# A batched matmul (A times B transposed) on one core: the last 256 KB of output stored in three transfers of unequal spread instead of inside one

## The chip, the cores and the metric

The kernel runs on one core of a Trainium2 chip. The metric is the device time of one execution in microseconds (us); lower is better. Before the change the median of 15 runs is 125.15 us (124.88 to 125.45).

## What is computed

Sixteen independent products of float32 matrices, each 512 by 512:

```python
batch, m, k, n = 16, 512, 512, 512
np.matmul(a, b.transpose(0, 2, 1)).astype(np.float32)
```

The inputs are 33.55 MB, the output is 16.78 MB.

## The kernel before

**Tiling and stages.** The batches are worked in eight pairs (`pairs`), and `J = 4` output rows of a batch belong to each of the 128 partitions: row `p * 4 + j` of a batch lies in partition `p`, place `j`. A load (L87) brings both batches of a pair of `a` or of `b`, 2 MB, into one of seven slots of `ld`; even numbers are `a`, odd ones `b`. DVE casts to bf16 (`ha`, `wa`, `hb`, `wb`), PE transposes against an identity into `tp` (L199), ACT and DVE bring the transposes to `ta` (L157) and `tb` (L144), PE multiplies into `ps` (L218), and ACT copies the product to `ob` (L177), one of seven slots of 128 partitions by 4 rows by 512 float32. So a partition's share of a batch is four rows of 2 KB, 8 KB that lie side by side in `ob` and in the output.

**Queues.** ACT issues all loads but number 1, which SP issues; after that SP issues the stores, one per batch, 1 MB each. ACT's loads and SP's stores are two queues over the same 16 DMA engines. SP waits for `s_out` ahead of each store; ACT raises it on the second batch of a pair, after its first and after its last copy, so that store `2u` may go when the first copy of batch `2u + 1` is done, and store `2u + 1` when its last is.

**The end of the program**, which the change touches. `store(n)` (L92 to L96) waits and issues one transfer of a whole batch, whose semaphore `s_st[n % 7]` rises by 16 when all of it has landed. The loop at L107 issues stores 0 to 14, inside a hand-ordered block that closes with a barrier of all engines (L40). A second block (L232 to L234) then makes ACT wait for the landings of stores 9 to 14, one `wait_ge` for each. The last store, of batch 15, is issued by SP outside the block (L236); it is tied to the block only in the order of issue, so SP issues it while ACT waits. Its landing is waited for by SP itself, in the program's closing section (L270). That closing wait of SP asks for two things: the landing of the last store, and a semaphore of ACT that ACT raises after its walk through its own waits and a drain (L232). After it come drains and two barriers of all engines.

Of the kernel before, what the change touches and what calls it, by code (L numbers as in the profile page):

```python
# [10 lines left out]
def kernel(  # L11
# [6 lines left out]
    nc = tc.nc  # L18
    P = 128
    batch, M, K = a.shape  # L20
    _, N, _ = b.shape
    J = M // P
# [7 lines left out]
    NO = 7  # L30
# [3 lines left out]
    def sbuf(name, shape, dtype):  # L34
        return ctx.enter_context(nc.sbuf_tensor(name, shape, dtype))

    def sem(name):
        return tc.alloc_semaphore(name)

    with tc.tile_critical(no_gpsimd_drain=True):  # L40
# [8 lines left out]
        ob = sbuf("ob", [P, NO, J, N], f32)  # L49
# [4 lines left out]
        s_ld = [sem(f"s_ld{i}") for i in range(NL)]  # L54
        s_st = [sem(f"s_st{i}") for i in range(NO)]

        s_go = sem("s_go")
        s_wa = sem("s_wa")
        s_wb = sem("s_wb")
# [9 lines left out]
        s_out = sem("s_out")  # L69
# [5 lines left out]
            out=ident[:], in_=ident[:], compare_op=mybir.AluOpType.not_equal, fill=1.0,  # L75
# [13 lines left out]
        def landed(n):  # L89
            return s_st[n % NO], 16 * (n // NO + 1)  # L90

        def store(n):  # L92
            nc.sync.wait_ge(s_out, n + 1)
            nc.sync.dma_start(
                out[n].rearrange("(p j) n -> p j n", j=J), ob[:, n % NO]
            ).then_inc(landed(n)[0], 16)  # L96

        load(0, nc.scalar)
        load(1, nc.sync)
# [4 lines left out]
            nc.gpsimd.wait_ge(s_ld[n % NL], 16 * (n // NL + 1)).then_inc(s_go, 1)  # L104

        nc.sync.wait_ge(s_ld[0], 32)
        for n in range(batch - 1):  # L107
            store(n)

        def taker(engine):  # L110
            return lambda s, n: engine.wait_ge(s, n).then_inc(s, -n)  # L111
# [9 lines left out]
        with nc.Fori(0, pairs, engines=[dve]) as u:  # L121
            for x, (h, w, s_c, s_w) in enumerate(
# [4 lines left out]
                if x == 0:  # L127
# [4 lines left out]
                    out=h[:, J:, :], in_=src[:, J:, :HK]  # L132
                ).then_inc(s_c, 1)
                nc.vector.tensor_copy(out=w[:], in_=src[:, :, HK:]).then_inc(s_w, 1)  # L134
            for ko in range(KO):
# [5 lines left out]
                if ko == 1:  # L141
# [3 lines left out]
                    out=tb[:, ko, :],  # L145
# [7 lines left out]
        for u in range(pairs):  # L153
            for ko in range(KO):
                nc.scalar.wait_ge(s_ta, KO * u + ko + 1)
                for e in range(2):
                    c = nc.scalar.copy(  # L157
                        out=ta[:, ko, e * J * P:(e + 1) * J * P].rearrange(
                            "k (j p h) -> k j p h", j=J, h=2
                        ),  # L160
# [10 lines left out]
            for e in range(2):  # L171
                n = 2 * u + e
                if n >= NO:
                    nc.scalar.wait_ge(*landed(n - NO))
                for j in range(J):
                    nc.scalar.wait_ge(s_mm, J * n + j + 1)
                    c = nc.scalar.copy(  # L177
                        out=ob[:, n % NO, j, :].rearrange("m (p j) -> m p j", j=2 * J),
# [51 lines left out]


    with tc.tile_critical(sync_engine=act, no_gpsimd_drain=True):  # L232
        for n in range(batch - NO, batch - 1):
            nc.scalar.wait_ge(*landed(n))  # L234
    waits = nc.cur_bb.bb.instructions[-1]
    last = nc.sync.dma_start(  # L236
        out[batch - 1].rearrange("(p j) n -> p j n", j=J), ob[:, (batch - 1) % NO]
    )
    tc.add_manual_dep(
        last.ins,  # L240
        waits.name,
# [33 lines left out]
```

## Time and profile before

| what | value |
|---|---|
| median of 15 runs | 125.15 us |
| the profiled execution, its own time | 125.18 us |
| its span, first to last instruction | 123.4 us (1.78 us of its time lie around it) |
| PE, PEld, DVE, ACT busy | 92.3, 57.4, 68.0, 68.0 us |
| moved by DMA | 50.34 MB, 408 GB/s over the span |
| share of 16 DMA engines' span, load queue and store queue | 60.5% and 36.3% |
| last copy to `ob` (L177) starts, lasts | 114.49 us, 0.59 us |
| store 14 and the last store issued by SP | 112.95 and 115.26 us |

PE is the TensorE matmul, DVE VectorE, ACT ScalarE, SP SyncE; a "q" behind an engine's name is its instruction sequencer, which waits and issues. The profile shows busy shares in 40 slices, the chain of work that ended last, groups of instructions by line, waits by who waited for whom, and the DMA share and rate in any stretch. The trace also holds every DMA packet with its start, length and size, though not the number of the engine that moved it, and the moment of every count of a store's semaphore.

### The profile page before, as it was taken

Reading aid. Unit: us, or ns where it says so; the run is one execution under the profiler, and the core shown is the slowest. Engines: PE = TensorE matmul, PEld = TensorE weight load, DVE = VectorE, ACT = ScalarE, POOL = GpSimd, SP = SyncE. Lnnn points to the kernel's source line nnn. Section 1 sums busy time; section 2 is a strip of 40 time slices with the busy share of each in tenths; the row PEclk is TensorE's granted clock in tenths of the full one; section 3 lists DMA queues with packets and bytes.
Section 4 is the critical chain, followed back from the end, with each engine's and each line's share of the span. In section 5 each row is a group of like instructions: output and inputs, shape, how many; then the busy total and the mean of one; then the engine's idle time right before and its main releaser. Section 6 shows DMA issues by size and latency. Waiting matters only on the chain. (4 is left out here: it accounts for less than half of the span.)

```text
span 123.4 us, 2235 instructions
## 1 busy us (share of the span) xinstructions
PE 92.3 (75%) x768; PEld 57.4 (47%) x768; DVE 68.0 (55%) x96; ACT 68.0 (55%) x130; POOL 0.7 (1%) x6
## 2 busy tenths in 40 slices
PE   0000089999899999989998999899899926999000
PEld 0000079546734774476467447634764515844000
DVE  0000598891898389568928991891977039510000
ACT  0400063557956885596679658946976093655300
POOL 2000000000000000000000000000000000000000
PEclk9999999999999999999999999999999998699955
DMA  4999999999999999999999999999999999999990
GB/s 122 398 430 441 430 425 425 441 425 436 425 425 425 425 398 388 446 422 436 420 428 446 409 422 452 406 452 430 414 446 420 414 422 428 428 425 422 433 422 19
DMA packets 4609, 50.34 MB, mean 408 GB/s; under 512 B 512, under 2 KB 512, under 8 KB 512
## 3 DMA queue, kind: packets, MB, share of 16 engines
q10 hardware_dynamic: 2160, 31.46, 60.5%
q1 hardware_dynamic: 2448, 18.88, 36.3%
q14 instruction: 1, 0.01, 0.0%
HBM read 33.55 MB, written 16.78 MB: 408 GB/s over the span
## 5 line engine op out<-in xcount | busy, mean ns | idle before, releaser
L218 PE MATMUL ps<-tb,ta 128*128 128x512 bf16 x256 | 57.7, 379 | 0.4
L177 ACT COPY ob<-ps 128x512 f32<-128x512 f32 x64 | 34.3, 591 | 27.3 <-PE ps L218 24.3
L157 ACT COPY ta<-tp 128x512 bf16<-128x512 bf16 x64 | 33.0, 613 | 15.8 <-PE tp L199 15.2
L218 PEld LDWEIGHTS ps<-tb,ta 128*128 128x128 bf16 x256 | 24.1, 98 | 30.5 <-issue 3.9
L199 PE MATMUL tp<-ident,ha 128*128 128x128 bf16 x256 | 20.3, 236 | 18.4 <-PEq L111 17.9
L199 PEld LDWEIGHTS tp<-ident,ha 128*128 128x128 bf16 x256 | 17.3, 106 | 22.0 <-issue 20.2
L144 DVE COPY tb<-tp 128x1024 bf16<-128x1024 bf16 x32 | 21.3, 685 | 5.2 <-DVEq L111 5.2
L199 PE MATMUL tp<-ident,hb 128*128 128x128 bf16 x256 | 18.8, 232 | 3.3 <-PEq L111 3.3
L199 PEld LDWEIGHTS tp<-ident,hb 128*128 128x128 bf16 x256 | 16.7, 105 | 4.0 <-issue 3.7
L130 DVE CAST ha<-ld 128x1024 bf16 x8 | 5.5, 690 | 14.7 <-POOLq L104 13.7
L139 DVE COPY ha<-wa 128x2048 bf16<-128x2048 bf16 x8 | 5.5, 691 | 12.7 <-DVEq L111 12.7
L134 DVE CAST wa<-ld 128x2048 bf16 x8 | 9.8, 1220 | 0.0
L134 DVE CAST wb<-ld 128x2048 bf16 x8 | 9.8, 1220 | 0.0
L130 DVE CAST hb<-ld 128x1024 bf16 x8 | 5.5, 688 | 7.5 <-DVEq L111 7.5
L143 DVE COPY hb<-wb 128x2048 bf16<-128x2048 bf16 x8 | 5.5, 685 | 0.1
L131 DVE CAST ha<-ld 128x1024 bf16 x8 | 5.5, 686 | 0.0
L131 DVE CAST hb<-ld 128x1024 bf16 x8 | 5.5, 686 | 0.0
L152 ACT ACT_TABLE_LOAD x1 | 1.3, 1283 | 4.0 <-issue 4.0
L74 POOL TENSOR_SCALAR_AFFINE_SELECT ident<-ident 128x128 bf16<-128x128 bf16 x1 | 0.3, 292 | 0.2 <-POOL ident L72 0.2
L72 POOL MEMSET ident<- 128x128 bf16 x1 | 0.2, 204 | 0.5 <-SPq L40 0.5
L152 ACT COPY one<-const-float32-1.0 128x1 f32<-128x1 f32 x1 | 0.2, 192 | 0.0
L259 POOL MEMSET const-bfloat16-1.0<- 128x1 bf16 x1 | 0.1, 101 | 0.0
(3 smaller groups left out, 0.3 us busy)
## 6 DMA issues: line engine op xcount, KB each, us to landing
ld<-in_a_dram ACTq DMA_DIRECT2D x8, 2048.0 KB, 28.3
out_dram<-ob SPq DMA_DIRECT2D x16, 1024.0 KB, 25.4
ld<-in_b_dram ACTq DMA_DIRECT2D x7, 2048.0 KB, 26.0
ld<-in_b_dram SPq DMA_DIRECT2D x1, 2048.0 KB, 12.5
```

The costliest lines, as they stand in the source:

```text
L74: nc.gpsimd.affine_select(out=ident[:], in_=ident[:], compare_op=mybir.AluOpType.not_equal, fill=1.0, base=0, pattern=[[-1, P]], channel_m ...
L130: nc.vector.tensor_copy(out=h[:, :J, :], in_=src[:, :J, :HK])
L131: nc.vector.tensor_copy(out=h[:, J:, :], in_=src[:, J:, :HK]).then_inc(s_c, 1)
L134: nc.vector.tensor_copy(out=w[:], in_=src[:, :, HK:]).then_inc(s_w, 1)
L139: nc.vector.tensor_copy(out=ha[:], in_=wa[:]).then_inc(s_ca, 1)
L143: nc.vector.tensor_copy(out=hb[:], in_=wb[:]).then_inc(s_cb, 1)
L144: nc.vector.tensor_copy(out=tb[:, ko, :], in_=tp[:, 2 + ko % 2].rearrange("k j p -> k (j p)"),).then_inc(s_eb, 1)
L152: nc.scalar.copy(out=one[:], in_=nc.const_aps.tensor(1.0, (P, 1), f32))
L157: c = nc.scalar.copy(out=ta[:, ko, e * J * P:(e + 1) * J * P].rearrange("k (j p h) -> k j p h", j=J, h=2), in_=tp[:, ko % 2, :, e * HP:(e ...
L177: c = nc.scalar.copy(out=ob[:, n % NO, j, :].rearrange("m (p j) -> m p j", j=2 * J), in_=ps[:, j, :].rearrange("m (j p) -> m p j", j=2 * J),)
L199: t = nc.tensor.transpose(tp[:, 2 * x + g, j, :], h[:, j, g * P:(g + 1) * P], ident[:])
L218: t = nc.tensor.matmul(ps[:, j, :], ta[:, ko, (e * J + j) * P:(e * J + j + 1) * P], tb[:, ko, :].rearrange("k (j p) -> k j p", j=2 * J)[:, ...
```

## The change

The first three rows of each partition of batch 15 now go as a transfer like the others, with the semaphore of their slot, at the end of the loop. The fourth row of each partition, 2 KB in each of 128 partitions, goes in three transfers by groups of partitions: 92 to 127 (36 partitions, over twelve DMA engines), 0 to 31 (32, over sixteen), both issued by SP at once behind the loop, each with a semaphore of its own, and 32 to 91 (60, over fifteen) as the last store, where the whole batch's stood. ACT's block of waits has three more: the landing of batch 15's first three rows, and of the two new transfers.

```diff
+        s_part = [sem(f"s_part{i}") for i in range(2)]
...
-        def store(n):
-            nc.sync.wait_ge(s_out, n + 1)
-            nc.sync.dma_start(
-                out[n].rearrange("(p j) n -> p j n", j=J), ob[:, n % NO]
-            ).then_inc(landed(n)[0], 16)
+        def store(n, lo=0, hi=J, part=slice(0, P)):
+            return nc.sync.dma_start(
+                out[n].rearrange("(p j) n -> p j n", j=J)[part, lo:hi], ob[part, n % NO, lo:hi]
+            )
...
-        for n in range(batch - 1):
-            store(n)
+        for n in range(batch):
+            nc.sync.wait_ge(s_out, n + 1)
+            store(n, hi=J if n < batch - 1 else J - 1).then_inc(landed(n)[0], 16)
+
+        for s, part in zip(s_part, (slice(92, P), slice(0, 32))):
+            store(batch - 1, lo=J - 1, part=part).then_inc(s, 16)
...
-        for n in range(batch - NO, batch - 1):
+        for n in range(batch - NO, batch):
             nc.scalar.wait_ge(*landed(n))
+        for s in s_part:
+            nc.scalar.wait_ge(s, 16)
     waits = nc.cur_bb.bb.instructions[-1]
-    last = nc.sync.dma_start(
-        out[batch - 1].rearrange("(p j) n -> p j n", j=J), ob[:, (batch - 1) % NO]
-    )
+    last = store(batch - 1, lo=J - 1, part=slice(32, 92))
```

## The prediction

> **What bounds the kernel now.** I read the page's slices first, then the end in fine windows, then who waits there. The slices:
>
> ```profile
> PE   0000089999899999989998999899899926999000
> ...
> DMA  4999999999999999999999999999999999999990
> GB/s 122 398 430 441 430 425 425 441 425 436 425 425 425 425 398 388 446 422 436 420 428 446 409 422 452 406 452 430 414 446 420 414 422 428 428 425 422 433 422 19
> ```
>
> The DMA engines are full from the second slice to the last but one at 390 to 450 GB/s, while PE has gaps at both ends. So the kernel is bound by its 50.34 MB, and a compute engine matters only if it starves the queues. At the end it can't: the last copy to `ob` ends at 115.08 us, the last store is issued at 115.26, and its first packets start at about 117.9, behind the stores before it. What is left is how the engines finish. Windows of the end (the columns after the clock, which is 0.50, are the DMA share and GB/s):
>
> ```profile
> 119.00:120.00 1.00, 0.00 (x0) 0.00 (x0) 0.00 (x0) 0.00 (x0) 0.00 (x0) 0.50 1.04 442
> ...
> 120.25:120.50 0.25, 0.00 (x0) 0.00 (x0) 0.00 (x0) 0.00 (x0) 0.00 (x0) 0.50 0.26 98
> ...
> 120.75:121.00 0.25, 0.00 (x0) 0.00 (x0) 0.00 (x0) 0.00 (x0) 0.00 (x0) 0.50 0.08 33
> ...
> 121.25:121.50 0.25, 0.00 (x0) 0.00 (x0) 0.00 (x0) 0.00 (x0) 0.00 (x0) 0.50 0.08 33
> 121.50:121.75 0.25, 0.00 (x0) 0.00 (x0) 0.00 (x0) 0.00 (x0) 0.00 (x0) 0.50 0.08 33
> ```
>
> 33 GB/s is one 8 KB packet in a quarter of a microsecond: from 120.75 on a single engine works. The trace's packets say the same. Fifteen engines end their data between 120.26 and 120.86; one **trailing engine** starts its last packet at 121.60 and ends it at 121.91, so it is 1.05 us behind the next. The counts of the last store follow: fifteen from 120.62 to 121.22, the sixteenth at 122.38. Store 14 has the same spread, 118.17 to 119.91. The end is then this:
>
> ```profile
> SPq L270 <- DMA out_dram<-ob: 6.7, 1, 6.7
> ...
> L270 SPq EVENT_SEMAPHORE  x1: 28/28/28, 122.4 to 122.4; - x1
> ```
>
> SP's closing wait lasts 6.7 us, ends at 122.40 with the trailing engine's count, and the drains and barriers behind it take 1.0 us to 123.4. The other condition of that wait, ACT's semaphore, was met long before. ACT's end (L234, then the lines of L270 and L232 on ACT's sequencer; count, length in ns, first and last start):
>
> ```profile
> L234 ACTq EVENT_SEMAPHORE  x1: 17/17/17, 119.9 to 119.9; - x1
> ...
> L270 ACTq EVENT_SEMAPHORE  x5: 38/38/38, 120.0 to 120.3; - x5
> L270 ACTq COMPARE_BRANCH  x1: 33/33/33, 120.4 to 120.4; - x1
> ...
> L232 ACTq DRAIN  x1: 14/14/14, 120.6 to 120.6; - x1
> ```
>
> This is the row that decides my forecast. L234 ends at 119.93, when store 14 lands (119.91). By its semaphore that is the wait for store 14, the one written **last** in the loop; the waits for stores 13, 12, 11, 10 and 9 come after it, in that reversed order, one to each of the five instructions of L270, which start 0.077 us apart, each together with a wait of the program's own. Then come the branch, an event at L232 and the drain that raises ACT's semaphore at 120.62. From the landing to there is 0.71 us. Before the change this walk is free: it ends 1.76 us ahead of the last store's landing.
>
> **The change part by part.**
>
> *Issues on SP.* One transfer becomes four: 3 more issues at 0.333 us (the row of L94 and L236) and some 0.05 between them. The first three rows go when the last copy is done, at about 115.1, the two parts at 115.5 and 115.9. Then SP arrives at the barrier of L40, at about 116.25 where it came at 113.32; DVE, PE, POOL and ACT wait there but have no work left. The last part goes at about 116.7. The engines need the parts only after the first three rows, from 119.6 on, and the part that is issued last not before 120.0. The cover is 3 us; the first load's packets came 1.04 us after its issue. Cost: nothing, and without the cover 1.2 us at most.
>
> *The packets.* A 16 KB packet takes 0.611 us and an 8 KB packet 0.309, so 8 KB cost 0.302 and a packet 0.007; it starts 0.003 before its predecessor ends. A 6 KB row group is then 0.231 and a 2 KB row 0.080 (an estimate; the trace has nothing between 4 B at 0.009 and 8 KB at 0.309, and these are its bounds). Before, the trailing engine has 8 packets of 8 KB in the last store, 8 x 0.306 = 2.45 us. After, it has 8 of 6 KB, 1.85, and its rows of the three parts: 36 / 12 = 3 rows if it is among the twelve, 2 of the sixteen for certain, 60 / 15 = 4 if it is among the fifteen. The trace doesn't number engines, so all combinations are open. What counts is the part over all sixteen (`s_part[1]`), which no engine escapes: without the twelve's rows ahead of it, it ends 1.85 + 0.16 = 2.01 us after the trailing engine starts batch 15, **0.44 earlier** than before, landing at 121.94; with them 0.24 later, at 122.19. The fifteen's rows stand behind it and end at 122.05 + 0.47 (from last packet to count, as before) = 122.5 at worst, and only SP waits for them.
>
> [...]
>
> *The other fifteen engines.* At most 9 rows in place of 8 quarter shares: 0.08 us, and two more count packets of 0.009. That brings the latest of them from 120.86 to about 120.96; the cover is the trailing engine's lag of 1.05 us. Reading 36 or 32 partitions at once instead of 128 may slow them: between nothing and, if two engines share what one had, a doubling of the nine rows, 0.72 us, to 121.68. I take nothing, as no row shows a slowing; even the doubling stays within the lag, so the sum doesn't change.
>
> [...]
>
> *ACT's waits.* Three more: batch 15's first rows, `s_part[0]`, `s_part[1]`. If the order is reversed as it is now, ACT stands at `s_part[1]`, whose last count is the trailing engine's, and everything else comes after it, satisfied but not free: the 0.71 of before, and three waits more, two to an instruction of 0.077: 0.08 to 0.15, I take 0.12. Together **0.83 us, now on the path**, since SP's closing wait asks for ACT's semaphore. Bounds of the walk: 0.33 if the new wait stands last (0.71 less five steps of 0.077), 0.94 if each new wait takes an instruction. I take 0.83 because the row shows the reversed order.
>
> *Sum.* 121.94 + 0.83 = 122.77, and 0.02 for SP to see it: 122.79 in place of 122.40, so +0.39 us. The span becomes 123.8 and the execution 125.18 + 0.39 = 125.57; the profiled execution is 0.03 over the median, so I forecast 125.55.
>
> **The rivals.**
>
> 1. *The trailing engine is one of the twelve.* For it: they are twelve of sixteen. Against it: nothing in this trace. `s_part[1]` lands at 122.19, the walk ends at 123.02, SP at 123.04: +0.64, 125.8.
> 2. *The waits are walked in the written order*, `s_part[1]` last, and all others are done by then. For it: the program is written so. Against it: L234, which shows store 14's wait first. Then 121.94 + 0.33 + 0.02 = 122.29, -0.11: 125.05, not slower. The point from which it decides is a walk of 0.44 us behind the landing, the gain of the packets: shorter is a gain, longer a loss.
> 3. *Faster.* As 2, and the trailing engine's count comes 0.36 us after its last packet, as the other engines' counts do, in place of 0.47, or its small rows cost less than I take: -0.22 to -0.35, 124.8 to 124.95. Against it: it needs both. With the reversed order it would need a landing 1.1 us earlier, and only 0.44 us of work is taken from the trailing engine.
> 4. *The change doesn't do what it says*: the parts spread otherwise, so that the trailing engine keeps 8 or 9 rows. That gives the price of 1.
>
> **How the numbers follow.** Forecast (the trailing engine outside the twelve, reversed walk) 0.58; rival 1 with 4 0.17; rival 2 0.15; rival 3 0.10. About 0.2%, 0.25 us, is what a measurement of this kernel can tell from no change; the forecast is 0.15 us beyond it, and with the walk's bounds and the rows' price I give it 0.85 of being slower by more. So slower 0.58 x 0.85 + 0.17 = 0.66, same 0.09 + 0.15 = 0.24, faster 0.10. The forecast's own range is 125.35 to 125.7 (walk 0.71 to 0.94, landing 121.9 to 122.0). The range for 8 in 10 leaves out rival 3 and the upper part of rival 1: 124.95 to 125.9.
>
> **What would show it.** In the profile after: SP's closing event (L270) at about 122.8, and before it on ACT one single wait that ends at 121.9 to 122.0, then six or seven events 0.077 apart; SP's wait ended by ACT and no longer by the DMA. The windows from 120.75 on should show smaller packets and the single engine done by about 121.5. Rival 1 shows that engine at work until 121.7 or later; rival 2 shows ACT's last event, not its first, ending with the landing. I am wrong if ACT's semaphore is raised within 0.4 us of the last landing, or if the trailing engine lands more than 0.8 us earlier.

## The result

The changed kernel takes 125.80 us (median of 9 runs, 125.68 to 126.13) against 125.16 before (47 runs, 124.86 to 125.67): ratio 1.0053, 95% interval 1.0042 to 1.0063, so 0.66 us longer, 0.53 to 0.79. A second set beside other kernels gave 1.0047 (1.0034 to 1.0061). The direction, and ACT's walk as the cause of it, were as forecast; the relief of the trailing engine was not there, and the size was that of the first rival (125.8) and not that of the forecast (125.55).

### The profile page after: what moved, and what is told of

Its sections match the earlier page's. It is cut to its first block, busy times and chain, and to the rows that moved or that the text cites. A ratio compares the mean times of both kernels' runs of the same rounds, so it can differ in the third digit from the quotient of the medians.

```text
span 123.8 us, 2239 instructions
## 1 busy us (share of the span) xinstructions
PE 91.0 (74%) x768; PEld 55.9 (45%) x768; DVE 67.9 (55%) x96; ACT 68.0 (55%) x130; POOL 0.7 (1%) x6
## 5 line engine op out<-in xcount | busy, mean ns | idle before, releaser
L203 PE MATMUL tp<-ident,ha 128*128 128x128 bf16 x256 | 19.0, 228 | 18.0 <-PEq L115 17.6
L203 PEld LDWEIGHTS tp<-ident,ha 128*128 128x128 bf16 x256 | 16.3, 102 | 21.5 <-issue 19.7
L203 PE MATMUL tp<-ident,hb 128*128 128x128 bf16 x256 | 18.3, 229 | 3.5 <-PEq L115 3.3
L203 PEld LDWEIGHTS tp<-ident,hb 128*128 128x128 bf16 x256 | 16.1, 103 | 4.4 <-issue 4.1
```

Of the source, the lines that this page charges most:

```text
L203: t = nc.tensor.transpose(tp[:, 2 * x + g, j, :], h[:, j, g * P:(g + 1) * P], ident[:])
```

## The profile after

The profiled execution took 125.59 us, span 123.8, so 0.41 over the profiled execution of before and 0.21 under the median of its own kernel. In the changed kernel L274 is the program's closing section (L270 before), L238 ACT's written waits (L234) and L236 the block around them (L232).

The DMA rows of the page, after (DMA busy tenths and GB/s in 40 slices):

```profile
DMA  4999999999999999999999999999999999999990
GB/s 106 397 439 429 429 429 434 445 429 434 424 429 424 424 392 408 432 413 455 408 424 455 410 439 432 410 445 424 434 429 421 426 429 424 426 421 426 432 375 9
```

Nothing changed up to the last two slices: the four issues on SP left no gap in the DMA engines. The end in windows, after:

```profile
119.00:120.00 1.00, 0.00 (x0) 0.00 (x0) 0.00 (x0) 0.00 (x0) 0.00 (x0) 0.50 0.98 399
120.25:120.50 0.25, 0.00 (x0) 0.00 (x0) 0.00 (x0) 0.00 (x0) 0.00 (x0) 0.50 0.74 279
120.75:121.00 0.25, 0.00 (x0) 0.00 (x0) 0.00 (x0) 0.00 (x0) 0.00 (x0) 0.50 0.06 25
121.25:121.50 0.25, 0.00 (x0) 0.00 (x0) 0.00 (x0) 0.00 (x0) 0.00 (x0) 0.50 0.07 25
121.50:121.75 0.25, 0.00 (x0) 0.00 (x0) 0.00 (x0) 0.00 (x0) 0.00 (x0) 0.50 0.07 25
121.75:122.00 0.25, 0.00 (x0) 0.00 (x0) 0.00 (x0) 0.00 (x0) 0.00 (x0) 0.50 0.02 8
```

Most of the other engines end a little later (279 GB/s from 120.25 on, where it was 98; the last of them ends at 120.82, at 120.86 before), and from about 120.8 one engine is alone, as before. 25 GB/s is three packets of 2 KB in a quarter of a microsecond: the trailing engine works on the fourth row until 121.84, where it was done at 121.91 before. The trace's packets give its share: after its last 6 KB packet (end 121.10) come 3 rows, a count, 2 rows, a count, 4 rows, a count. **It has all three parts**, nine rows of 2 KB in place of eight quarters. The counts land at 121.84 (`s_part[0]`), 122.05 (`s_part[1]`) and 122.30 (the last store). It is the rows that show the share, not the moment: in changed_again's trace below the engine has the same 3, 2 and 4 rows, but is less behind there (store 14 lands at 119.46, 119.71 here), and `s_part[1]` lands at 121.81.

Who waits, after: first a line of the waits of SP, then ACT's end and SP's closing events (count, lengths in ns, first and last start):

```profile
SPq L274 <- ACTq L236: 5.7, 1, 5.7
```

```profile
L238 ACTq EVENT_SEMAPHORE  x2: 38/38/38, 121.9 to 122.1; - x2
...
L274 ACTq EVENT_SEMAPHORE  x5: 38/38/38, 122.1 to 122.5; - x5
L274 ACTq COMPARE_BRANCH  x1: 32/32/32, 122.5 to 122.5; - x1
...
L236 ACTq DRAIN  x1: 8/8/8, 122.8 to 122.8; - x1
...
L274 SPq EVENT_SEMAPHORE  x1: 480/480/480, 122.3 to 122.3; - x1
```

The releaser of SP's closing wait was the last store and is now ACT. SP stands 0.48 us in that wait after its own transfer has landed (122.30), from 122.32 to 122.80. In that time ACT walks: its second written wait, `s_part[1]`, ends at 122.07; then follow the five events, the branch, an event and the drain, 0.72 us from the landing to ACT's semaphore at 122.77.

## The experiments

Theory A: the loss is ACT's walk, which now begins when the last part lands, and the trailing engine isn't relieved. Theory B: the loss is in the transfers, by small packets, few partitions at once or more issues. Ratios are to the kernel before, run beside on the same chip.

**walk_alone**: the walk without the parts. All stores are whole and in the loop, there is no last store outside it.

```diff
-        for n in range(batch - 1):
+        for n in range(batch):
             store(n)
...
-        for n in range(batch - NO, batch - 1):
+        for n in range(batch - NO, batch):
             nc.scalar.wait_ge(*landed(n))
```

> All sixteen stores are issued whole in the loop and ACT's block waits for all seven last landings; no transfer is split, and SP has no last store of its own to wait for. Theory A (the loss is ACT's walk through its waits, which now begins only when the last transfer lands): the landing stays where it was before, at 122.4 us of the span, and the walk of 0.72 us, as it stood behind the landing of s_part[1] in the changed kernel (122.05 to 122.77), follows it: 0.7 over before, about 125.85. Theory B (the loss is in the transfers: small packets, fewer partitions at once, four issues): nothing is split, so 125.15 to 125.25.

Measured: 1.0058 (1.0042 to 1.0075), 0.73 us over. Its SP waits, and the end of ACT:

```profile
SPq L260 <- ACTq L232: 8.4, 1, 8.4
```

```profile
L234 ACTq EVENT_SEMAPHORE  x1: 38/38/38, 122.3 to 122.3; - x1
...
L232 ACTq DRAIN  x1: 8/8/8, 123.0 to 123.0; - x1
```

The whole store lands at 122.32, as before within 0.06; ACT's semaphore comes at 123.04, 0.72 later. No transfer is split and the loss is there: theory B is out as the main cause.

**parts_alone**: the parts without the walk. The kernel before, with its last store replaced by the changed kernel's four transfers, all outside ACT's block:

```diff
-    last = nc.sync.dma_start(
-        out[batch - 1].rearrange("(p j) n -> p j n", j=J), ob[:, (batch - 1) % NO]
-    )
+    for lo, hi, p0, p1 in ((0, 3, 0, 128), (3, 4, 92, 128), (3, 4, 0, 32), (3, 4, 32, 92)):
+        last = nc.sync.dma_start(
+            out[batch - 1].rearrange("(p j) n -> p j n", j=J)[p0:p1, lo:hi],
+            ob[p0:p1, (batch - 1) % NO, lo:hi],
+        )
```

> The same four transfers as in the changed kernel, but all issued behind ACT's block, where the last store stood, so that SP waits for their landings and ACT waits for stores 9 to 14 only, as before. Theory A: the walk is off the path again; the trailing engine moves the same bytes in more packets (nine rows of 0.080 us for eight quarters of 0.305, and three more counts, +0.13 us), and SP's closing wait is one or two events of 0.07 longer: 0.1 to 0.25 over before, about 125.3. Theory B: as slow as the changed kernel, about 125.8.

Measured: 1.0017 (1.0005 to 1.0028), 0.21 us over. SP's waits and events at the end:

```profile
SPq L272 <- DMA out_dram<-ob: 4.8, 3, 4.4
```

```profile
L272 SPq EVENT_SEMAPHORE  x3: 28/28/28, 122.0 to 122.4; - x3
```

SP waits for the DMA again, and its last event comes at 122.44, 0.02 after the last landing (122.43). The trailing engine has 3, 2 and 4 rows here too. So the split costs a little and gains nothing: its relief isn't there.

**waits_turned**: the changed kernel with ACT's waits written the other way round.

```diff
-        for n in range(batch - NO, batch):
-            nc.scalar.wait_ge(*landed(n))
-        for s in s_part:
-            nc.scalar.wait_ge(s, 16)
+        for s in reversed(s_part):
+            nc.scalar.wait_ge(s, 16)
+        for n in reversed(range(batch - NO, batch)):
+            nc.scalar.wait_ge(*landed(n))
```

> The changed kernel with ACT's nine waits written in the opposite order, so that s_part[1] is the last to be walked. Theory A: 0.33 us stand behind the landing of s_part[1] in place of 0.72, which is only 0.07 later than SP sees the landing of the last transfer (0.26 behind s_part[1]): about 0.4 under the changed kernel, 125.4. Theory B: the order of waits is nothing, 125.8 as changed.

Measured: 1.0031 (1.0017 to 1.0045), 0.39 us over before. Its five last waits on ACT, and the drain that raises ACT's semaphore:

```profile
L274 ACTq EVENT_SEMAPHORE  x5: 173/610/2417, 116.5 to 121.8; - x5
...
L236 ACTq DRAIN  x1: 8/8/8, 122.2 to 122.2; - x1
```

The waits are now spread over the last transfers (up to 2.4 us in one of them, waiting for a landing) and not strung behind them. `s_part[1]` lands at 121.94 and ACT's semaphore comes at 122.24, 0.31 later; the last store lands at 122.19, so SP would have stood there almost as long anyway. The point estimate is 0.27 us under the changed kernel's, for a new order of nine lines; the two intervals meet at 1.0042 to 1.0045, and the two were not run side by side.

**which_engine**: which engine trails? Changed kernel, parts of other sizes (with a third semaphore in `s_part`):

```diff
-        for s, part in zip(s_part, (slice(92, P), slice(0, 32))):
+        for s, part in zip(s_part, (slice(0, 7), slice(7, 15), slice(15, 80))):
...
-    last = store(batch - 1, lo=J - 1, part=slice(32, 92))
+    last = store(batch - 1, lo=J - 1, part=slice(80, P))
```

> The fourth row of each partition goes in parts of 7, 8, 65 and 48 partitions, whose largest divisors up to sixteen are 7, 8, 13 and 16. If a part runs on that many engines from the lowest-numbered on, the trailing engine's 2 KB packets tell its place: 1, 1, 5, 3 rows if it is among the first seven, 0, 1, 5, 3 if it is the eighth, 0, 0, 5, 3 if it is the ninth to thirteenth, 0, 0, 0, 3 if it is one of the last three. The changed kernel's trace shows 3, 2 and 4 rows on it, so it is not one of the last four, by this rule. One look; the time is not the question.

Measured (a single execution, 125.54): the trailing engine's packets are 8 of 6 KB, then 1, 1, 5 and 3 rows. It is one of the seven engines of the smallest part.

**which_engine_2**: as parts_alone, with other parts:

```diff
+    for lo, hi, p0, p1 in ((0, 3, 0, 128), (3, 4, 0, 1), (3, 4, 1, 3), (3, 4, 3, 7), (3, 4, 7, 128)):
```

> As which_engine, with parts of 1, 2, 4 and 121 partitions (over 1, 2, 4 and 11 engines by their divisors), issued behind ACT's block so that the walk is off the path. The rows on the trailing engine, which is among the lowest seven, tell more: 1, 1, 1, 11 if it is the first, 0, 1, 1, 11 the second, 0, 0, 1, 11 the third or fourth, 0, 0, 0, 11 the fifth to seventh. Eleven rows in place of eight make it 0.24 to 0.5 later than before. One look.

Measured (a single execution, 125.49, on another chip): its rows are 0, 0, 0 and 11, and its trace has 530 count packets, 18 more than that of the kernel before, as many as 1, 2, 4 and 11 engines make. The trailing engine is not one of the four, and it is one of the eleven. If it is the same engine in both runs and the parts nest, it is the fifth, sixth or seventh in the order in which they take engines in. In the changed kernel's trace they nest: its packets after the 6 KB ones, linked where one begins 2 to 6 ns before another ends, make sixteen engines, of which twelve have 3, 2 and 4 rows, three 2 and 4, and one 2. That the smaller parts here do so too was not shown. A number is a place in that order: no trace gives an engine's own.

**even_parts** and, beside the changed kernel, **even_parts_again**: all three parts over sixteen engines.

```diff
-        for s, part in zip(s_part, (slice(92, P), slice(0, 32))):
+        for s, part in zip(s_part, (slice(80, P), slice(0, 48))):
...
-    last = store(batch - 1, lo=J - 1, part=slice(32, 92))
+    last = store(batch - 1, lo=J - 1, part=slice(48, 80))
```

> The changed kernel with its three parts over all sixteen engines each: partitions 80 to 127 (48), 0 to 47 (48) and 48 to 79 (32, the last store), so that every engine has 3, 3 and 2 rows, the eight quarters it had before. Theory A (the trailing engine has all three parts, and ACT's walk stands behind s_part[1]): s_part[1] comes after 6 rows and not 5, so 0.08 later, and the rest is as changed: 125.75 to 125.9. Rival C (the unequal spread relieves the trailing engine, and the loss would be greater without it, by the six rows of 0.08): 126.2. Rival D (fewer partitions or fewer engines at once cost time): under the changed kernel by 0.2 or more, 125.5.

> The changed kernel as it is, beside the next run on one chip: 0.5% over before, as it was.

> even_parts once more, beside the changed kernel. Theory A: 0.0 to 0.1 us over the changed kernel. Rival D (fewer engines or partitions at once cost time): 0.2 or more under it.

Measured: even_parts 1.0043 (1.0018 to 1.0068); even_parts_again 1.0046 (1.0032 to 1.0060) beside 1.0047 (1.0034 to 1.0061) for the changed kernel. The spread over twelve, sixteen and fifteen engines makes no difference that these runs can tell: it doesn't relieve the trailing engine (rival C asked for about 1.008), and no cost of it is seen (rival D asked for 1.0031 or less, just under the second interval but inside the first, so a small cost is not excluded).

**pool_share**: a try to relieve it. Behind ACT's block, rows 0 and 1 in one transfer, rows 2 and 3 in parts, two of them issued by POOL:

```diff
+    for engine, lo, hi, p0, p1 in (
+        (nc.gpsimd, 2, 4, 0, 7), (nc.gpsimd, 2, 4, 7, 70), (nc.sync, 0, 2, 0, 128),
+        (nc.sync, 2, 4, 70, 80), (nc.sync, 2, 4, 80, 128),
+    ):
```

> A try to relieve the trailing engine in earnest. Rows 2 and 3 of the last batch (4 KB pieces of 0.155 us) go in parts: 7 and then 63 partitions issued by POOL, 10 and 48 by SP; rows 0 and 1 of all partitions by SP; all behind ACT's block, so that SP waits for the landings. If POOL's transfers take their engines in turn from where the last one stopped (7 engines, then the nine others), the first seven engines have 1 + 3 + 1 = 5 pieces and the nine others 10 or 11, in place of 8: the trailing engine ends 3 x 0.155 = 0.46 earlier, less 0.1 for counts and closing events, 124.8 against 125.15 before. If POOL's parts lie otherwise, or POOL's way of issuing costs something at the end, 125.3 to 126.

Measured: 1.0011 (0.9998 to 1.0025). The plan gave the trailing engine one piece of POOL's first transfer and none of its second. The trace shows otherwise: the last landing of the first transfer is at 121.53, and after that the engine that works alone to the end (122.63) still moves POOL pieces, at 121.83 and 122.00, in front of its count for the second (last landing 122.78). So the engines of the second transfer were not the nine others; nothing was relieved.

**four_engines**, **four_engines_again** and **four_last**: the relief where which_engine and which_engine_2 put the trailing engine, as parts_alone with other parts. four_last has the part of 60 partitions first (0 to 59) and that of 68 last (60 to 127).

```diff
+    for lo, hi, p0, p1 in ((0, 3, 0, 128), (3, 4, 0, 68), (3, 4, 68, 128)):
```

> A try to relieve the trailing engine where which_engine and which_engine_2 put it, fifth to seventh by number: the fourth row goes in two parts, partitions 0 to 67 (68, largest divisor up to sixteen is 4, so 17 rows on each of four engines) and 68 to 127 (60, 4 rows on each of fifteen), both behind ACT's block with the first three rows, so that SP waits for the landings and no walk is on the path. If the four engines are the lowest, the trailing engine has 4 rows in place of 8, 0.32 earlier, less 0.05 for counts and a closing event; the four engines have 13 rows more, 1.04, which brings them from 120.3 to 120.9 to at most 121.3 to 121.9, about where the trailing engine then ends. 124.85 to 125.1 where before is 125.15; if the four engines are the later ones among the fifteen, no gain or 0.1 over.

> four_engines once more. Its executions fell in two groups, 7 near 124.83 and 4 from 125.14 to 125.76; the trace of one of the latter shows the trailing engine done at 121.49 (relieved, 4 rows), and an engine of the four, 0.6 us late at the start of its part, done at 122.62 with its 21 rows. If that is the cause, two groups again, 124.8 to 124.9 whenever none of the four is late; as a whole 0.1 to 0.3 under before.

> The same parts in the other order: partitions 0 to 59 over fifteen engines first, 60 to 127 over four last. Each engine moves the same rows, so the time is that of four_engines, in two groups; if the order of the parts matters by itself, another.

Measured: 0.9991 (0.9978 to 1.0004), 1.0006 (0.9984 to 1.0029) and 0.9991 (0.9971 to 1.0010): not told apart from the kernel before. The trailing engine was relieved in all three traces, but what the four others had more came out as late. In the first, windows of the end:

```profile
121.25:121.50 0.25, 0.00 (x0) 0.00 (x0) 0.00 (x0) 0.00 (x0) 0.00 (x0) 0.50 0.24 90
121.50:121.75 0.25, 0.00 (x0) 0.00 (x0) 0.00 (x0) 0.00 (x0) 0.00 (x0) 0.50 0.09 33
121.75:122.00 0.25, 0.00 (x0) 0.00 (x0) 0.00 (x0) 0.00 (x0) 0.00 (x0) 0.50 0.06 25
122.00:122.25 0.25, 0.00 (x0) 0.00 (x0) 0.00 (x0) 0.00 (x0) 0.00 (x0) 0.50 0.06 25
122.25:122.50 0.25, 0.00 (x0) 0.00 (x0) 0.00 (x0) 0.00 (x0) 0.00 (x0) 0.50 0.07 25
```

In the 90 GB/s the trailing engine still has its share, and is done at 121.48 with four rows; the engine that is alone from 121.75 on is one of the four. It started its 21 rows 0.7 to 0.9 us later than the other three, just behind a 6 KB packet of 0.680 us in place of 0.234; two of its rows took 0.176 and 0.235 us in place of 0.084, and it ended at 122.62 (that execution took 125.76). Why these packets were slow stays open. In the other two traces one of the four ends its data last as well, at 121.74 and 121.69. In four_engines_again its count is the last landing, at 122.06; in four_last the last landing is still that of the trailing engine, whose four rows end at 121.64 and whose count comes at 122.11. That is 0.32 and 0.27 earlier than before (122.38); those executions took 124.89 and 125.00. The times of four_engines fell in two groups, 7 of 11 from 124.80 to 124.90; the two groups did not come back in the two later runs, which spread from 124.84 to 126.04, and the kernel before spread as widely beside them (124.77 to 125.83). Nothing run here is shown to beat the kernel before.

## Why the prediction was right in direction and short in size

- **What bounds the end**: right. The DMA engines are full (9 tenths busy or more in 38 of 40 slices, before and after), and in every trace but the three with the relief the trailing engine alone sets the last landing.
- **Issues on SP at no cost**: right in effect, wrong in price. The issues behind the first took 1.00, 0.86 and 0.57 us, not 0.333, and the last part went at 116.43, near the 116.7 that I wrote, because the last copy ended 1.4 us earlier in this execution (113.66). The cover of 3 us held: the packets follow one another without a gap.
- **Price of the packets**: right. In the changed kernel's trace a 2 KB packet took 0.084 us and the next began 0.080 after its start; a 6 KB packet 0.234 and 0.231.
- **The trailing engine's share**: this is the step that failed. I put it outside the twelve with 0.58 against 0.17, with no row of the trace for it: 2, 5, 6 or 9 rows were open, and I took the reading that gave the relief, though twelve of sixteen engines lie among the twelve. It has all nine rows, so the 0.44 us that I took off its work are not taken off. By the working of rival 1, `s_part[1]` then lands 0.25 later than in the forecast, and that rival's time of 125.8 is the one measured. In part this is luck too: with the walk as it was measured (0.72, below), the same sum gives 0.53 over before, 125.7, at the lower end of the measured interval. The late counts of `s_part[0]`, `s_part[1]` and the last store in the changed kernel's trace, twelve, sixteen and fifteen, are the numbers of engines that the change was written for.
- **The other fifteen**: right that they stay within the lag. A slowing by fewer partitions at once isn't seen: nearly all 2 KB packets took 0.084 (0.086 at most in the changed kernel), those of the part from partitions 0 to 31 too.
- **ACT's walk**: right in kind, 0.11 too long. The waits for stores 13 to 9 came last and in reversed order, as read from L234, and SP waited for ACT. But I added 0.12 for three more waits, and none of it stands behind the landing: the waits for batch 15's first rows and for `s_part[0]` make up the first instruction, `s_part[1]` shares the second with store 14's wait (so the wait written last is walked second, not first), and the five events behind are those of before. 0.72, not 0.83.
- **The sum in the trace** came out by luck, through two errors: SP's event at 122.80 where I wrote 122.79, with the walk 0.11 shorter, the landing 0.11 later (122.05 for 121.94). The landing would have been later still, but it seems that this execution's trailing engine was less behind: store 14's counts spread over 1.56 us, 1.74 in the trace of before. So the profiled execution shows 0.41 and the medians 0.66.
- **The account from the experiments**: parts 0.21 (0.06 to 0.35), walk 0.72, less 0.26, as the last store lands that much after `s_part[1]` and SP would wait for it anyway: 0.67, against 0.66 measured. The interval of the first term alone is wider than that agreement.

Open: why one engine trails, and whether it is the same one on every chip. The counts of store after store show its lag, not its cause (in the kernel before, the last count of stores 11 to 15 came 1.06 to 1.17 us behind the one ahead of it); every trace read shows a trailing engine, and none contradicts a fixed place. That it is at one place on all of them is not shown.

## What to carry to other kernels

Here a wait added at the end of the program was not priced by its own 0.04 us but by everything that its engine still had to walk once it was released, 0.72 us: look which wait comes first in the trace, and let the last landing be waited for by the engine that has the least left to do. Before work is taken from "the slow engine", find out from packets or counts which one it is: in these runs a spread that was cut by divisors of the partition count relieved only the engines that were left out, and the trailing one was not among them until its rows had been counted. And when a profiled execution agrees with a forecast, check the terms one by one; two may be off in opposite directions.

## What the runs showed that was not expected

- Issuing a transfer straight behind another often held SP for 0.75 to 1.1 us (1.00 and 0.86 in the changed kernel), where a single store's issue took 0.33; others took 0.30 to 0.65. The number of partitions doesn't set it: 0.99 us for 7 partitions and 0.93 for 65 in which_engine; in which_engine_2 transfers of 1 and 2 partitions took 0.35 and 0.34, that of 4 took 1.05 and that of 121 behind it 0.30. The cause wasn't looked for.
- The order in which waits are written on one engine shows in the trace, since this program walked them nearly in reverse: ACT's semaphore comes 0.72 us behind the landing of `s_part[1]` one way, 0.31 the other. That the time of the kernel gains by it (0.27) is likely but not shown, as the two intervals meet.
- The count of a store landed some time after the engine's last packet, and that time wasn't fixed. In the last store of the kernel before it was 0.47 us on the trailing engine and 0.36 on the others. In the changed kernel the trailing engine's counts took 0.46 to 0.53, but the last of the others took 0.52 as well (120.82 to 121.34).
